# One decoder layer (Conformer mixer and gated conv-FFN): shift and scale vectors summed on VectorE, two pointwise-1 tiles per step, one LayerNorm token tile in the convolution's banks

## The chip, the cores and the metric

The kernel runs on one core of a Trainium2 chip. The metric is the device time of one execution in microseconds (us); lower is better.

## The reference, cut to what matters

One layer (DEPTH 1) of a decoder trunk, 1024 tokens by 1024 channels, everything in float32. Six vectors of 1024 values are made from `c`: shift, scale and gate for the mixer, and shift, scale and gate for the FFN.

```python
c_act = jax.nn.silu(c)
mod = c_act @ mod_w[i] + mod_b[i]                      # 1024 x 6144
sh_m, sc_m, gt_m, sh_f, sc_f, gt_f = jnp.split(mod, 6, axis=-1)
h = rmsnorm(x, norm_pre_mix[i]) * (1.0 + sc_m) + sh_m
u = h @ w1 + b1                                        # pointwise 1: 1024 -> 2048
a, gt = jnp.split(u, 2, axis=-1)
u = a * jax.nn.sigmoid(gt)                             # GLU
u = causal_dwconv(u, dw_w) + dw_b                      # depthwise, 31 taps
u = jax.nn.silu(layernorm(u, ln_g, ln_b))
y = u @ w2 + b2                                        # pointwise 2
x = x + gt_m * rmsnorm(y, norm_post_mix[i])
h = rmsnorm(x, norm_pre_ffn[i]) * (1.0 + sc_f) + sh_f
y = conv_ffn(h, ...)                                   # 1024 -> 5632, 3 taps, gate, 2816 -> 1024
x = x + gt_f * rmsnorm(y, norm_post_ffn[i])
```

## The kernel before

**Tiling.** The tokens are cut into two blocks of 512 (b = 0, 1), each of four token tiles of 128, and the channels into eight tiles of 128. A large matmul is done in three passes (`mm3`, lines 256 to 260): every operand is split into a high part and a remainder (`split`, line 241; the high part by ScalarE at L244 or VectorE at L246, the remainder by VectorE or GpSimd at L247), and high x high, high x low and low x high are added up in one PSUM bank. A matmul of 128x512 is one of the three passes.

**Memory.** PSUM has eight banks: six of the pool `bank` and two of the pool `cbank`, which the convolution accumulates in. Split weights live in four buffers `W` of 128x1024 (`pw`), so two pointwise-1 tiles' worth: each channel tile j of pointwise 1 takes two, one for the values and one for the gate. Raw weights have three buffers, `Q` tiles of 128x512 three, `Y` tiles of 128x1024 eight, `A` tiles twenty.

**The front.** `load_norm(0)` (L274) loads block 0's four token tiles, squares them on ScalarE with an accumulated sum, and scales them. Then the mixer's shift and scale come from `c` one channel tile k at a time: `channel_vectors(k)` (L137) loads two 512 KB tiles of `mod_w`; `channel_partials` (L146) multiplies them on TensorE by silu(c), eight matmuls of 128x256 in four column groups, and ScalarE copies the result; `channel_sums` (L157) adds the partitions up with two more matmuls and finishes `sh_m` and `s_m` on VectorE. `modulate_T(.., k)` (L263) transposes the normalised tokens, applies scale and shift on ScalarE, and splits the result. `pw1_step` (L296) runs the six matmuls of channel tile k for output tile j = 0. Lines 764 to 783 lay this out: all 16 tiles of `mod_w` are loaded before the weights of j = 1.

**Mixer.** Lines 801 to 823 run pointwise 1 for j = 1 to 7 of block 0 and for block 1's j = 4 to 7, 0 and 1. `glu` makes the gated result and `conv` (L335) the depthwise convolution: 7 of 31 taps go to ScalarE and GpSimd, 23 to VectorE (L355), accumulated in a `cbank`. Block 0's taps are put off in the text (`late`, L361, run at L825), while the compiler's scheduler lays the instructions of each engine in an order of its own, by readiness and then by place in the text. `ln_norm(cs0, t)` (L368) transposes one token tile of the convolution's output into two banks (L374), takes its statistics (L375) and normalises it; `ln_back` (L387) transposes back. `pointwise2` (L454) follows, with the sandwich norms in its `evacuate` (L465 to L486).

**The FFN's vectors.** `todo` (L809) holds six pieces (p, h): the mixer's gate (p = 0), the FFN's shift (p = 1) and scale (p = 2), each in two halves. `pieces()` (L787) loads four 512 KB tiles of a piece, multiplies them on TensorE (`piece_partials`, L173, matmuls at L179), and then either spreads the result over rows (`into_rows`, L224) or sums it into channel layout (`into_channels`, L186, matmuls at L190). The FFN's gate is summed on VectorE later (`row_sums`, L202 to L211).

**FFN.** `modulate_block(xs, s_f, sh_f)` (L843) needs `sh_f` and `s_f` and starts the FFN of block 0, in whose course VectorE also convolves block 1. Block 1's FFN ends with `down_strassen` (L654), whose last step accumulates each output tile into `yacc` (L664), squares it (L669), multiplies by the norm's weight (L670) and calls `finish` (L740). All DMAs go through the SP queue in order.

These lines set the order of the front:

```python
xs = load_norm(0)
ws = pw1_weights(0, DV)
chunk = [channel_vectors(k) for k in range(KD)]
...
for k in range(KD + 1):
    if k + 1 < KD:
        part.append(channel_partials(chunk[k + 1]))
    if k < KD:
        channel_sums(k, *part[k])
        hT[0][k] = modulate_T(xs, s_m, sh_m, k)
    if k > 0:
        pw1_step(bks, ws, hT[0][k - 1], k - 1)
```

## Time and profile before

| | us |
|---|---|
| median of 3 runs (lowest to highest) | 1088.54 (1087.88 to 1088.59) |
| the profiled execution | 1087.78 |
| its span, from the first to the last instruction | 1086.0 |
| TensorE busy in the span | 1059.2 (98%) |
| VectorE busy | 820.2 (76%) |
| GpSimd busy | 509.7 (47%) |
| ScalarE busy | 499.6 (46%) |

PE is TensorE's matmul stream and PEld its weight loads, DVE is VectorE, ACT ScalarE, POOL GpSimd, SP the queue that issues the DMAs. "out<-in" names tiles by the program's names. A row of grouped instructions gives its count, the busy time, the mean of one in ns, and the idle time of the engine just before them with what ended it. Matmuls overlap in the pipeline, so the time a matmul costs is the distance from its start to the next one's, not the duration in its row; the same holds on a smaller scale for the other engines. A row of the timeline gives the start, the length, the engine, the line, the operation and the count of instructions merged into it. Lines are those of the kernel before.

### The profile page before, as it was taken

The page shows a single profiled execution, that of the slowest core. Times are in us where ns is not written, and L with a number is a line of the kernel's source. Part 1 is how long each engine was busy: PE and PEld are TensorE (multiplying, and loading weights), DVE is VectorE, ACT ScalarE, POOL GpSimd, SP SyncE. Part 2 cuts the span into 40 slices and gives each one's busy share as a digit, 9 for nine tenths or more (in the row PEclk, how much of TensorE's full clock was granted, in tenths as well). Part 3 has the DMA queues.
Part 4 walks back from the last instruction along what each step waited for, and adds up shares of the span by engine and source line. Part 5 has one row for each costly group of instructions (what it writes and reads, how often), then busy time and mean ns, then how long its engine had stood idle before and what let it go on. Part 6 is the DMA issues. An engine that isn't in the chain of part 4 may idle for free.

```text
span 1086.0 us, 13033 instructions
## 1 busy us (share of the span) xinstructions
PE 1059.2 (98%) x4786; PEld 836.6 (77%) x4786; DVE 820.2 (76%) x1127; ACT 499.6 (46%) x774; POOL 509.7 (47%) x380
## 2 busy tenths in 40 slices
PE   5999999999999999999999999999999999999996
PEld 3678876778788888888887788888887888878884
DVE  3499989533899999989978673786596555965588
ACT  4495555453644544324444432455445444443443
POOL 2398876544644444444444363223257023650464
PEclk9999999999999999999999999999999999999999
DMA  9951135443422233342343253567204323033122
GB/s 377 368 195 59 59 117 194 155 135 98 155 78 97 97 97 97 93 167 90 97 166 93 92 155 97 174 213 271 91 26 155 117 97 97 20 118 116 39 77 79
DMA packets 41831, 139.00 MB, mean 128 GB/s; under 512 B 4644, under 2 KB 4644, under 8 KB 41768
## 3 DMA queue, kind: packets, MB, share of 16 engines
q1 hardware_dynamic: 41768, 138.18, 37.2%
q8 instruction: 37, 0.61, 0.2%
q14 instruction: 26, 0.21, 0.1%
HBM read 129.77 MB, written 8.39 MB: 127 GB/s over the span
## 4 chain that ended last, share of the span: by engine, by line
PE 88%; DVE 5%; DMA 3%; ACT 2%; issue 1%; POOL 1%; SPq 0%; DVEq 0%; ACTq 0%; POOLq 0%
PE bank L259 26%; PE bank L260 26%; PE bank L258 26%; PE bank L636 2%; PE bank L637 2%; PE bank L635 2%; DMA raw<-in_w 1%; PE bank L179 1%; DVE W L247 1%; DMA Af<-in_mod_ch 1%; DMA Y<-in_mod_ch 1%; DVE R L699 1%; DVE yacc L664 1%; ACT W L244 0%; DVE n L462 0%
## 5 line engine op out<-in xcount | busy, mean ns | idle before, releaser
L259 PE MATMUL bank<-A,W 128*128 128x512 f32 x960 | 379.1, 395 | 1.7 <-DVE A L247 1.7
L258 PE MATMUL bank<-A,W 128*128 128x512 f32 x960 | 378.4, 397 | 1.0 <-DVE A L246 0.7
L260 PE MATMUL bank<-A,W 128*128 128x512 f32 x960 | 378.6, 395 | 0.0
L247 POOL TENSOR_TENSOR W<-raw,W 128x1024 fp32r<-128x1024 f32 x99 | 244.4, 2470 | 271.0 <-ACT W L244 228.5
L355 DVE SCALAR_TENSOR_TENSOR cbank<-U,vecs,cbank 128x512 f32<-128x512 f32 x424 | 290.9, 749 | 9.0 <-ACT cbank L343 7.8
L258 PEld LDWEIGHTS bank<-A,W 128*128 128x128 f32 x960 | 180.1, 188 | 49.2 <-issue 1.9
L259 PEld LDWEIGHTS bank<-A,W 128*128 128x128 f32 x960 | 180.5, 188 | 45.9 <-DVE A L247 2.5
L260 PEld LDWEIGHTS bank<-A,W 128*128 128x128 f32 x960 | 180.5, 188 | 43.6 <-issue 0.8
L244 ACT ACTIVATE W<-raw 128x1024 fp32r<-128x1024 f32 x150 | 157.9, 1053 | 113.9 <-PE bank L260 71.7
L534 ACT ACTIVATE U<-bank,vecs 128x512 f32<-128x512 f32 x88 | 68.3, 778 | 193.9 <-PE bank L260 193.6
L535 DVE SCALAR_TENSOR_TENSOR U<-bank,vecs,U 128x511 f32<-128x511 f32 x88 | 65.4, 746 | 79.6 <-ACT U L534 79.4
L258 PE MATMUL bank<-W,A 128*128 128x512 f32 x304 | 121.0, 398 | 0.0
L259 PE MATMUL bank<-W,A 128*128 128x512 f32 x304 | 120.2, 395 | 0.0
L260 PE MATMUL bank<-W,A 128*128 128x512 f32 x304 | 119.0, 395 | 0.0
L540 POOL TENSOR_TENSOR U<-U,hv 128x2 f32<-128x2 f32 x44 | 12.7, 288 | 153.0 <-DVE U L535 150.0
L247 DVE TENSOR_TENSOR W<-raw,W 128x1024 fp32r<-128x1024 f32 x51 | 62.2, 1221 | 19.1 <-ACT W L244 19.1
L247 DVE TENSOR_TENSOR A<-U,A 128x512 fp32r<-128x512 f32 x73 | 69.3, 962 | 8.2 <-ACT A L244 7.7
L353 POOL TENSOR_TENSOR Q<-Q,Q 128x512 f32<-128x512 f32 x48 | 62.2, 1296 | 15.9 <-ACT Q L349 14.9
L259 PEld LDWEIGHTS bank<-W,A 128*128 128x128 f32 x304 | 57.2, 188 | 13.7 <-issue 0.5
L258 PEld LDWEIGHTS bank<-W,A 128*128 128x128 f32 x304 | 57.2, 188 | 13.7 <-issue 0.5
L260 PEld LDWEIGHTS bank<-W,A 128*128 128x128 f32 x304 | 57.2, 188 | 13.4
L536 DVE SCALAR_TENSOR_TENSOR U<-bank,vecs,U 128x510 f32<-128x510 f32 x88 | 65.3, 744 | 1.6
(154 smaller groups left out, 1188.1 us busy)
## 6 DMA issues: line engine op xcount, KB each, us to landing
raw<-in_wup SPq DMA_DIRECT2D x88, 512.0 KB, 3.2
raw<-in_w SPq DMA_DIRECT2D x40, 512.0 KB, 3.8
Y<-in_mod_hp SPq DMA_DIRECT2D x32, 512.0 KB, 5.9
raw<-in_wdn SPq DMA_DIRECT2D x22, 512.0 KB, 3.6
R<-in_wdn SPq DMA_DIRECT2D x20, 512.0 KB, 3.8
Af<-in_mod_ch SPq DMA_DIRECT2D x12, 512.0 KB, 10.2
Y<-in_x SPq DMA_DIRECT2D x8, 512.0 KB, 10.0
U<-in_x SPq DMA_DIRECT2D x16, 256.0 KB, 3.7
```

What stands on the lines that cost most here:

```text
L244: nc.scalar.activation(dst[:, 0], src, AF.Copy)
L247: split_lo[0] = lo.tensor_tensor(dst[:, 1], src, dst[:, 0].bitcast(F32), op=ALU.subtract)
L258: nc.tensor.matmul(o, l[0], r[0], start=start, stop=False)
L259: nc.tensor.matmul(o, l[0], r[1], start=False, stop=False)
L260: nc.tensor.matmul(o, l[1], r[0], start=False, stop=stop)
L353: nc.gpsimd.tensor_tensor(acp, acp, q, op=ALU.add)
L355: nc.vector.scalar_tensor_tensor(acc, ut[:, k:k + 512], tap(k), acc, op0=ALU.mult, op1=ALU.add)
L534: nc.scalar.activation(t[:, :512], bk, AF.Identity, bias=V("fb", i), scale=wk[2])
L535: nc.vector.scalar_tensor_tensor(t[:, 1:512], bk[:, 0:511], wk[1], t[:, 1:512], op0=ALU.mult, op1=ALU.add)
L536: nc.vector.scalar_tensor_tensor(t[:, 2:512], bk[:, 0:510], wk[0], t[:, 2:512], op0=ALU.mult, op1=ALU.add)
L635: nc.tensor.matmul(o, l[0], r[0], start=start, stop=False, skip_group_check=group)
L636: nc.tensor.matmul(o, l[0], r[1], start=False, stop=False, skip_group_check=group)
```

## The change

- The FFN's and the mixer's shift and scale no longer go through TensorE. `mod_w` is laid out transposed in memory, so that a tile holds 128 output channels on its partitions and all 1024 inputs along the row. silu(c) is spread over all partitions as a row (`silu_row`, or two PSUM banks in `silu_banks`), made from Sigmoid and a multiplication. A VectorE instruction multiplies a tile by that row and adds up along it (`accum_out`): two of 1024 per channel tile for the mixer (`channel_sums`), 32 of 512 for the FFN (`ffn_sums`, loaded through the three `Q` buffers, placed in the text behind `pointwise2(0, ..)`). ScalarE finishes `sh_m` and `s_m`.
- The front loads the weights of j = 0 first, those of j = 1 behind the first two channel tiles of `mod_w`, and runs pointwise 1 for j = 0 and j = 1 in the same steps (four banks). Two of the four squares of `load_norm(0)` move to VectorE, and the high part of `modulate_T` in the front to ScalarE. `load_norm(1)` moves behind the GLU of j = 1 on VectorE.
- Four of the six pieces (p = 1, 2) are gone from `todo`.
- `ln_norm` takes the convolution's two banks for token tile 2.
- At the end of block 1's FFN the last sum of a tile is written to a PSUM bank, and squared and multiplied there, rather than in `yacc`.

The diff, cut to its core (a line of "..." marks what is left out):

```diff
@@ trunk_kernel
-    nc.scalar.activation(cz[:, :, 0], V("c", 0, KD), AF.Silu)
+    sg_c = cst.tile([P, KD], F32, name="sg_c")
+    nc.scalar.activation(sg_c, V("c", 0, KD), AF.Sigmoid)
+    nc.vector.tensor_tensor(cz[:, :, 0], sg_c, V("c", 0, KD), op=ALU.mult)
...
+    def silu_row():
+        row, sg = tY(), tAf().rearrange("p a b -> p (a b)")
+        dma[0] = nc.sync.dma_start(row, rows[5:6, :].to_broadcast([P, D]))
+        def use():
+            nc.scalar.activation(sg, row, AF.Sigmoid)
+            nc.vector.tensor_tensor(row, row, sg, op=ALU.mult)
+            return row
+        return use
...
-    def channel_partials(ws):
...
-    def channel_sums(k, bk, part):
+    def channel_sums(k, ws, row):
+        d = small(2, "dot")
         for g in range(2):
-            nc.tensor.matmul(bk[:, 256 + g:257 + g], part[:, g * P:(g + 1) * P], ones[:, 0:1], start=True, stop=True)
-        nc.vector.tensor_tensor(sh_m[:, k:k + 1], bk[:, 256:257], V("mb_shm", k), op=ALU.add)
-        nc.vector.scalar_tensor_tensor(
-            s_m[:, k:k + 1], bk[:, 257:258], scb[:, 0, k:k + 1], V("pre_mix", k), op0=ALU.add, op1=ALU.mult)
+            nc.vector.scalar_tensor_tensor(
+                ws[g], ws[g], 1.0, row, op0=ALU.mult, op1=ALU.mult, accum_out=d[:, g:g + 1])
+        nc.scalar.activation(sh_m[:, k:k + 1], d[:, 0:1], AF.Identity, bias=V("mb_shm", k))
+        nc.scalar.activation(s_m[:, k:k + 1], d[:, 1:2], AF.Identity, bias=scb[:, 0, k:k + 1], scale=V("pre_mix", k))
...
+    def silu_banks():
+        cs = []
+        for h in range(2):
+            q, c = tQ(), cbank()
+            nc.sync.dma_start(q, rows[5:6, h * 512:(h + 1) * 512].to_broadcast([P, 512]))
+            nc.scalar.activation(c, q, AF.Sigmoid)
+            nc.vector.tensor_tensor(c, c, q, op=ALU.mult)
+            cs.append(c)
+        return cs
+
+    def ffn_sums(cs):
+        d = sm.tile([P, 2, 2, KD], F32, tag="dots", name=nm("dots"), bufs=1)
+        for k in range(KD):
+            for p in range(2):
+                for h in range(2):
+                    q = tQ()
+                    nc.sync.dma_start(q, mod_cf[k, p, :, h * 512:(h + 1) * 512])
+                    nc.vector.scalar_tensor_tensor(
+                        q, q, 1.0, cs[h], op0=ALU.mult, op1=ALU.mult, accum_out=d[:, p, h, k:k + 1])
+            if k % 4 == 3:
+                ks = slice(k - 3, k + 1)
+                for p, fin in ((0, fin_sh), (1, fin_s)):
+                    nc.vector.tensor_tensor(d[:, p, 0, ks], d[:, p, 0, ks], d[:, p, 1, ks], op=ALU.add)
+                    fin(d[:, p, 0, ks], ks)
...
@@ load_norm
+            if b == 0 and t % 2 == 0:
+                nc.vector.scalar_tensor_tensor(junk, xt, 1.0, xt, op0=ALU.mult, op1=ALU.mult, accum_out=ss)
+            else:
+                nc.scalar.activation(junk, xt, AF.Square, accum_out=ss)
...
@@ ln_norm
-            bk = bank()
+            bk = cbank() if t == 2 else bank()
...
@@ down_strassen
+        def close(o, t, h, z):
+            hs = slice(h * 512, (h + 1) * 512)
+            if not last:
+                return accumulate(o, t, hs, False)
+            nc.vector.tensor_tensor(z, o, yacc[t][:, hs], op=ALU.add)
+            nc.scalar.activation(yacc[t][:, hs], z, AF.Square, accum_out=ns[t][:, h:h + 1])
+            nc.vector.tensor_tensor(z, z, g_f[:, hs], op=ALU.mult)
+            zs[t, h] = z
...
@@ the order of the front
+    ws = [pw1_weights(0, DV)]
     xs = load_norm(0)
-    ws = pw1_weights(0, DV)
-    chunk = [channel_vectors(k) for k in range(KD)]
+    silu_c = silu_row()()
+    chunk = [channel_vectors(k) for k in range(2)]
+    ws.append(pw1_weights(1, DV, tY()))
+    chunk += [channel_vectors(k) for k in range(2, KD)]
...
-    bks = [bank(), bank()]
-    part = [channel_partials(chunk[0])]
+    bks = [[bank(), bank()] for _ in range(2)]
     for k in range(KD + 1):
-        if k + 1 < KD:
-            part.append(channel_partials(chunk[k + 1]))
         if k < KD:
-            channel_sums(k, *part[k])
-            hT[0][k] = modulate_T(xs, s_m, sh_m, k)
+            channel_sums(k, chunk[k], silu_c)
+            hT[0][k] = modulate_T(xs, s_m, sh_m, k, hi=nc.scalar)
         if k > 0:
-            pw1_step(bks, ws, hT[0][k - 1], k - 1)
-    glu(0, 0, bks)
-    cs0 = [conv(0, 0, POOL_TAPS)]
+            for j in range(2):
+                pw1_step(bks[j], ws[j], hT[0][k - 1], k - 1)
+    cs0 = []
+    for j in range(2):
+        glu(0, j, bks[j])
+        cs0.append(conv(0, j, POOL_TAPS))
+    with tc.issue_after(last_glu[0].ins):
+        xs = load_norm(1)
...
-    for j in range(1, KD):
+    for j in range(2, KD):
...
-            into = [(early_m, use_m), (None, into_channels(fin_sh)), (None, into_channels(fin_s))]
-            todo = [(p, h) for p in range(3) for h in range(2)]
-        if j == 1:
-            xs = load_norm(1)
+            into = [(early_m, use_m)]
+            todo = [(0, h) for h in range(2)]
...
     zs += [ln_norm(cs0, t) for t in range(2, NT)]
+    silu_c = silu_banks()
     pw1_half(1, ws, bks, 1)
...
     xs = pointwise2(0, vs, b2, g_m, x2d)
+    ffn_sums(silu_c)
     pw1(1, SHARED - 1)
     h2 = modulate_block(xs, s_f, sh_f)
```

## Rows read from the trace of the kernel before

**Rows 1.** The page, part 1: each engine's busy time, share and instruction count.

```profile
PE 1059.2 (98%) x4786; PEld 836.6 (77%) x4786; DVE 820.2 (76%) x1127; ACT 499.6 (46%) x774; POOL 509.7 (47%) x380
```

**Rows 2.** The waits on TensorE: total us, times, longest.

```profile
PE bank L267 <- DVE Y L286: 10.2, 4, 7.9
PE bank L267 <- DVE Y L486: 2.0, 1, 2.0
```

**Rows 3.** Stretches: length, each engine's busy us (x count), PE clock, DMA share, GB/s.

```profile
200.00:250.00 50.00, 49.90 (x275) 39.51 (x274) 15.15 (x39) 23.60 (x31) 20.71 (x17) 1.00 0.35 115
250.00:300.00 50.00, 47.78 (x219) 38.37 (x218) 35.54 (x53) 25.61 (x50) 25.87 (x17) 1.00 0.37 126
...
450.00:500.00 50.00, 50.00 (x216) 40.24 (x215) 45.84 (x70) 16.25 (x21) 21.66 (x9) 1.00 0.39 133
```

**Rows 4.** TensorE's timeline around one piece of the FFN's vectors.

```profile
191.10 0.95 PE L190 MATMUL bank<-ones,U 128*128 128x1 f32 x8
191.98 1.92 PE L179 MATMUL bank<-Y,cz 128*32 128x512 f32 x16
193.83 0.50 PE L258 MATMUL bank<-A,W 128*128 128x512 f32 x1
```

**Rows 5.** TensorE's groups from 0 to 67.6 us.

```profile
L258 PE MATMUL bank<-A,W 128*128 128x512 f32 x48 | 18.2, 410 | 0.7 <-DVE A L246 0.7
L267 PE MATMUL bank<-ident,Y 128*128 128x128 f32 x40 | 7.2, 310 | 10.2 <-DVE Y L286 10.2
```

**Rows 6.** ScalarE's timeline: the first modulated tile; the GLU of j = 2.

```profile
17.61 0.78 ACT L269 ACTIVATE U<-bank,sh_m,s_m 128x512 f32<-128x512 f32 x1
...
67.82 0.69 ACT L304 ACTIVATE U<-bank,vecs 128x512 f32<-128x512 f32 x1 [0.55 <-PE bank L260]
```

**Rows 7.** TensorE's timeline: the first matmuls of pointwise 1.

```profile
19.52 0.73 PE L258 MATMUL bank<-A,W 128*128 128x512 f32 x2
```

**Rows 8.** The chain that ended last: start, length (issue to landing of DMAs).

```profile
4.13 8.38 DMA Y<-in_mod_ch
...
22.77 11.67 DMA raw<-in_w
```

**Rows 9.** The page, part 5: groups of instructions over the whole span.

```profile
L247 POOL TENSOR_TENSOR W<-raw,W 128x1024 fp32r<-128x1024 f32 x99 | 244.4, 2470 | 271.0 <-ACT W L244 228.5
L355 DVE SCALAR_TENSOR_TENSOR cbank<-U,vecs,cbank 128x512 f32<-128x512 f32 x424 | 290.9, 749 | 9.0 <-ACT cbank L343 7.8
...
L244 ACT ACTIVATE W<-raw 128x1024 fp32r<-128x1024 f32 x150 | 157.9, 1053 | 113.9 <-PE bank L260 71.7
...
L247 DVE TENSOR_TENSOR W<-raw,W 128x1024 fp32r<-128x1024 f32 x51 | 62.2, 1221 | 19.1 <-ACT W L244 19.1
```

**Rows 10.** Line 210 alone: ns min/median/max of one, first and last start.

```profile
L210 DVE SCALAR_TENSOR_TENSOR U<-Y,cz,U x16: 736/751/2360, 552.7 to 586.4; 128x512 f32<-128x512 f32 x16
```

**Rows 11.** ScalarE's groups from 0 to 56.5 us: reading an accumulator.

```profile
L284 ACT ACTIVATION_READ_ACCUMULATOR Af<-Y 128x1 f32 x8 | 1.5, 187 | 0.0
```

**Rows 12.** VectorE's timeline: block 0's convolution, its first and last instructions; the second norm.

```profile
56.65 2.34 DVE L355 SCALAR_TENSOR_TENSOR cbank<-U,vecs,cbank 128x512 f32<-128x512 f32 x3 [0.98 <-ACT cbank L343]
...
200.14 0.69 DVE L357 TENSOR_TENSOR U<-cbank,Q 128x512 f32<-128x512 f32 x1
...
266.96 0.70 DVE L471 TENSOR_TENSOR bank<-bank,b 128x512 f32<-128x512 f32 x1 [8.74 <-PE bank L260]
...
288.44 1.57 DVE L486 TENSOR_SCALAR Y<-Y,n 128x1024 f32<-128x1024 f32 x1 [0.66 <-POOL n L463]
```

**Rows 13.** TensorE's timeline: the first transposes of LayerNorm.

```profile
207.82 1.97 PE L374 MATMUL bank<-ident,U 128*128 128x128 f32 x16
```

**Rows 14.** DMA issues by group: count, KB each, median us from issue to landing.

```profile
U<-in_x SPq DMA_DIRECT2D x16, 256.0 KB, 3.7
...
U<-x2d SPq DMA_DIRECT2D x16, 256.0 KB, 3.2
```

**Rows 15.** VectorE's timeline at the end: the last tiles' multiplications.

```profile
1077.56 1.51 DVE L670 TENSOR_TENSOR yacc<-yacc,g_f 128x512 f32<-128x512 f32 x1 [0.19 <-ACT bank L669]
```

More of the change, by code (lines that the diff above doesn't have):

```diff
@@ L47, in trunk_kernel @@
 @with_exitstack
-def trunk_kernel(ctx, tc, x, vec, rows, mod_ch, mod_hp, w1, w2, wup, wdn, out):
+def trunk_kernel(ctx, tc, x, vec, rows, mod_ch, mod_cf, mod_hp, w1, w2, wup, wdn, out):
     nc = tc.nc
@@ L184, in piece_partials @@
         return part
-    def into_channels(fin):
-        def use(part, h):
-            b = bank()
-            for q in range(4):
-                nc.tensor.matmul(b[:, q:q + 1], part[:, q * P:(q + 1) * P], ones[:, 0:1], start=True, stop=True)
-            fin(b[:, 0:4], slice(4 * h, 4 * h + 4))
-        return use
     def fin_sh(b, ks):
@@ L247, in split, with weights @@
         split_lo[0] = lo.tensor_tensor(dst[:, 1], src, dst[:, 0].bitcast(F32), op=ALU.subtract)
-    def weights(src, lo=nc.gpsimd):
-        raw = pr.tile([P, 1024], F32, tag="raw", name=nm("raw"))
+    def weights(src, lo=nc.gpsimd, raw=None):
+        if raw is None:
+            raw = pr.tile([P, 1024], F32, tag="raw", name=nm("raw"))
         dma[0] = nc.sync.dma_start(raw, src)
@@ L291, in trunk_kernel, with pw1_weights @@
     tail = cst.tile([P, KD, PAD], F32, name="tail")
-    def pw1_weights(j, lo=nc.gpsimd):
-        return weights(w1[j], lo), weights(w1[KD + j], lo)
+    def pw1_weights(j, lo=nc.gpsimd, raw=None):
+        return weights(w1[j], lo), weights(w1[KD + j], lo, raw)
     def pw1_step(bks, ws, h, k):
@@ L652, in down_raw, with down_strassen @@
         return raws
-    def down_strassen(ci, lo, n, ops, raws, yacc, ns=None, done=None):
+    def down_strassen(ci, lo, n, ops, raws, yacc, zs, ns=None, done=None):
         last = done is not None
@@ L726, in down_strassen, with end @@
         for t in range(2):
-            accumulate(X[t], t + 2, D2, False)
-            final(t + 2, 1, tU()[:, :512])
-        def end(banks, dt, ds, h):
+            close(X[t], t + 2, 1, cbank() if last else None)
+        def end(banks, dt, h):
             def f(t):
-                accumulate(banks[t], t + dt, ds, dt == 0)
-                final(t + dt, h, banks[t])
+                if ci == 0 and dt == 0:
+                    accumulate(banks[t], t, D2, True)
+                else:
+                    close(banks[t], t + dt, h, banks[t])
                 if last:
@@ L736, in end, with finish @@
             return f
-        sweep("A22", lambda i: raws[i][2][1, 0], Q, False, True, V, end(Q, 2, D1, 0))
-        sweep("S4", lambda i: raws[i][2][1, 1], X, False, True, V if last else G, end(X, 0, D2, 1))
-    def finish(b, yacc, ns, x2d, split_halves=True):
+        sweep("A22", lambda i: raws[i][2][1, 0], Q, False, True, V, end(Q, 2, 0))
+        sweep("S4", lambda i: raws[i][2][1, 1], X, False, True, V if last else G, end(X, 0, 1))
+    def finish(b, yacc, ns, x2d, split_halves=True, zs=None):
         def done(t):
@@ L889, in trunk_kernel @@
         ns = [small(8, "n3") for _ in range(NT)] if last else None
-        down_strassen(ci, lo, n, ops, raws, yacc, ns, finish(1, yacc, ns, x2d) if last else None)
+        zs = {}
+        down_strassen(ci, lo, n, ops, raws, yacc, zs, ns, finish(1, yacc, ns, x2d, True, zs) if last else None)
 def _layout(i):
```

46 lines of the change are left out of this document (18 added, 28 removed).

## The prediction

> **What bounds the kernel now.** I read the engines' busy time first: TensorE is busy for 98% of the span, no other engine for more than 76% [rows 1]. The waits on TensorE come next: the longest are 10.2 us for the first normalised tokens and 2.0 us for the second norm of block 0 [rows 2]. So TensorE's instruction stream sets the time, and a saving is what leaves that stream, as long as no other engine lets it run dry. The stretches show where another engine is near: VectorE has 15 of 50 us busy from 200 to 250 us and 36 from 250 to 300, but 46 from 450 to 500 [rows 3]. In that last stretch 216 matmuls take 50.00 us, so one pass of 128x512 costs 0.2315 us [rows 3]. The profiled execution took 1087.78 us, 1.78 more than its span; the median of the runs is 0.76 above it.
>
> **Pieces removed.** One piece costs TensorE 0.88 us at L190 (191.10 to 191.98) and 1.85 us at L179 (to 193.83) [rows 4]. Four pieces leave: 4 x 2.73 = 10.9 us, from a stream that has no gap there. Their four 512 KB loads each are exchanged for 32 loads of 256 KB, the same 8 MB.
>
> **The front, before.** Up to 67.6 us, just before the GLU of j = 2 [rows 6], TensorE has run 48 matmuls of each pass (the rows of the other two passes have the same count), which is j = 0, 1 and 2, and 40 transposes, 8 of them block 1's [rows 5]. Taking away j = 2 (48 x 0.2315 = 11.1 us) and 8 transposes of about 0.11 us, the work of j = 0 and 1 is done at 55.6 us.
>
> **The front, after.** Three engines feed one another; I follow channel tile k = 7.
> Transfers: the first tile of `mod_w` lands at 12.51 us, the weights sixteen transfers later at 34.44, so 512 KB take 1.37 us [rows 8]. In the new order the silu row takes that first place, and 15 tiles of `mod_w` and two of weights lie between it and the last tile: 12.51 + 18 x 1.37 = 37.2 us.
> VectorE: a dot product of 1024 is not in the trace. Its nearest row is the two-input subtraction of 128x1024, 1.22 us [rows 9]; below, I bound it by 1.13 (that row less the overlap of neighbours), above by 1.41, with an accumulator read as on ScalarE, 0.19 [rows 11]. I take 1.25. From about 15 us, when the silu row is multiplied, VectorE has 16 of these (20.0), 8 remainders of about 0.62 (5.0) and two remainders of weights (2.4): it ends at 42.4 us, the last dot product at 41.8. That is later than the transfers allow, so VectorE sets the pace.
> Then ScalarE's two small finishing steps (0.3), 1.9 us from scale-and-shift to the first matmul as at 17.61 to 19.52 [rows 6, 7], and 12 matmuls (2.8): 46.8 us. Static orders of three engines never mesh; I add 0.2 us per channel tile, 1.7 in all: 48.5.
> A new gap follows. The four weight buffers are all in use until k = 7, so j = 2's first weights are split only then: ScalarE 1.05 and GpSimd 2.47 [rows 9], against 2.1 us of remaining matmuls and 0.5 that need the high part alone. About 1.0 us.
> So 49.5 instead of 55.6: **-6.1 us**. With dot products at 1.13 and no order loss it is 45 (-10); at 1.41 and twice the order loss 54 (-2). The 128 partial and 32 summing matmuls of the front are inside this term, not beside it.
>
> **LayerNorm.** VectorE convolves block 0 from 56.65 us to 200.8 [rows 12]. The start moves to about 50.2 with the GLU, and four scalings of block 1's tokens (2.7 us) come behind it: the end moves to about 197. TensorE reaches the first transposes at 207.8 [rows 13]; less 6.1, three L179 and two L190 blocks it would be there at 194.4. So it would wait 2.7 us, unless half a pointwise-1 tile (5.6 us) that lies behind is put ahead. I take +1, bounds 0 and 3. The fourth pair of banks lets three token tiles go at once; TensorE had other work there, so I give it nothing.
>
> **The FFN's sums.** 32 instructions of 512 against a PSUM bank: 0.67 us apart like L355's (0.75 in its row) [rows 9], 21.4 us, or 27 with a read of 0.19 each [rows 11]. With three buffers the transfers set a pace too: 3.2 to 3.7 us to landing [rows 14] plus 0.75 and some 0.1 of signals, over three: 1.35 to 1.5 us each, 43 to 49 us. They can start at about 208, when LayerNorm's third tile has left the two banks, and are done by 251 to 257. They are needed when block 0's second norm is done, which ran from 266.96 to 290 [rows 12] and now ends near 273. So they fit, beside some 16 us of other VectorE work (15 in the first of the two stretches [rows 3]); what they cost is waits in VectorE's order, where an evacuation stands behind a sum whose tile has not landed, and weights standing on SP behind a load that waits for its buffer. I take +2 us, bounds 0 and 16: the upper end is VectorE's other work, not overlapped at all.
>
> **The end.** The last multiplication of `yacc` took 1.51 us [rows 15], twice the 0.75 that L355 takes for as many elements [rows 9]; in PSUM it has one SBUF input like L355, which keeps that time beside a busy GpSimd. I take -0.5, bounds -0.8 and +0.5.
>
> **Edits at nothing.** The two squares, the sigmoid of `c` and the bank of token tile 2 lie beside the transfers of the first 15 us; without that cover they would cost some 3 us. Scale and shift finished on ScalarE are in the chain above.
>
> **Sum.** -10.9 - 6.1 + 1 + 2 - 0.5 = -14.5: 1087.78 becomes 1073.3, on the median's footing 1074.
>
> **A rule that speaks against the change.** L210 is the same instruction with two SBUF inputs of float32, without the sum: its median is 0.751 us, no longer than L355's 0.749 with one input in PSUM, though its longest took 2.36 beside a busy GpSimd [rows 9, 10]. The Trainium skill, "Vector Engine (DVE) Microarchitecture Reference", section "Points that are easy to get wrong", has it that this instruction with two SBUF sources that are not bf16 runs at half throughput, as no port is left for the accumulator. By that the mixer's dot products would take twice as long, and the row without accumulation cannot exclude it.
>
> **The rivals.**
> VectorE becomes the bound between LayerNorm and the FFN. If sums come at 1.5 us each and the splits, evacuations and norms queue behind them, the last sum comes at 257, seven us behind the first evacuation of the second half (266.96 less 17), and with two waits between them the second norm ends some 9 us late, and pointwise 1 of j = 3 is all that TensorE has left. For it: [rows 12] show a chain of 23 us there already, and [rows 2] a wait at its end. Against it: [rows 3], with 49 of 100 us idle. Time: 1083.
> Dot products of 1024 at half rate: 16 x 1.2 = 19 us more on the engine that paces the front: 1093. For it nothing here but the 2.36; against it the median.
> Slower, by one mechanism: VectorE's order keeps `ffn_sums` where the text has it, behind the second norm. Then the first sum starts at about 273 and, TensorE's filler used up, it waits for 32 x 1.2 = 38 us: 1112; it decides as soon as more than 12 of the sums lie behind that norm. Against it: block 0's taps, in the text behind all of pointwise 1, start at 56.65 [rows 12], so the order follows readiness.
> The change doesn't do what it says: waits refill every slot, the conversions' gaps included: 1088.
>
> **Chances.** Forecast 0.62 (1067 to 1081); VectorE as bound 0.18; half rate 0.05; sums behind the norm 0.07; no change 0.04; better than 1067, 0.04. A difference of about 0.2% (2.2 us) is what a measurement of this kernel can tell from none. Faster: 0.62 + 0.17 + 0.04 = 0.83; within: 0.05; slower: 0.12. The range leaves out the slower cases, no change and the best: 1066 to 1086, where the first rival's upper end lies.
>
> **What would show it.** Right: j = 1's GLU near 49 us; no L190 left and 32 records of L179; TensorE with under 4 us of waits at LayerNorm and at the FFN's first transposes; the last sum before 260 us. Wrong: a dot product of 1024 over 1.5 us; a wait of TensorE over 5 us for `s_f` or for a split behind a sum; weights landing late behind a load of `Q`.

## The result: slower by 0.7%, and the profile after

The changed kernel takes **1096.45 us** (median of 4 runs, 1094.54 to 1098.5) beside 1088.21 us of the kernel before on the same chip: ratio 1.0073, 95% interval 1.0059 to 1.0087. The forecast was 1074, with a range that ended at 1086. The profiled execution took 1098.5 us, the longest of the four, so the profiles account for 10.7 us where the medians differ by 8.2.

The page, part 1, of the changed kernel [rows 1]:

```profile
PE 1044.3 (95%) x4530; PEld 832.0 (76%) x4530; DVE 865.7 (79%) x1214; ACT 502.0 (46%) x784; POOL 499.3 (46%) x378
```

TensorE is busy for 14.9 us less, as meant, yet the span is 10.7 us longer: its idle time grew by 25.6 us. Its waits from 20 to 330 us, as total, times, longest [rows 2]:

```profile
PE bank L295 <- DVE Y L317: 5.7, 1, 5.7
PE bank L286 <- ACT A L271: 5.6, 1, 5.6
PE bank L286 <- ACT Y L417: 5.1, 1, 5.1
PE bank L295 <- DVE Y L519: 4.6, 3, 2.1
PE bank L295 <- DVE Y L515: 2.4, 2, 2.2
```

In the order of time, these are the first modulated tokens (second row), block 1's first transposes (first row), the LayerNorm of block 0 (third) and the second norm of block 0 (the last two). The stretches show where TensorE thinned out, 450 to 500 us being untouched [rows 3]:

```profile
60.00:80.00 20.00, 14.04 (x66) 11.57 (x65) 19.96 (x26) 12.29 (x20) 15.64 (x14) 0.83 0.26 87
200.00:250.00 50.00, 43.69 (x210) 35.65 (x210) 29.97 (x68) 23.73 (x32) 24.57 (x21) 0.93 0.57 186
250.00:300.00 50.00, 43.16 (x184) 33.86 (x182) 40.53 (x85) 20.23 (x43) 21.53 (x15) 0.94 0.61 209
450.00:500.00 50.00, 50.00 (x216) 40.52 (x216) 46.02 (x70) 14.35 (x17) 21.64 (x9) 1.00 0.41 137
```

**A ledger.** A three-pass matmul is three matmuls of 128x512, called passes here. Every kernel runs the same 4254 passes in the same numbers per stage, so the start of the n-th one can be compared with the n-th of the kernel before. Each entry is that difference in us, from the profiled executions (+ is later). Pass 96 ends the front (j = 0 and 1), 144 stands before block 1's first transposes and 168 behind them, 696 before the last half of a pointwise-1 tile at the LayerNorm, 768 behind it, 1008 behind the second norm.

| kernel | 96 | 144 | 168 | 696 | 768 | 960 | 1008 | 4254 |
|---|---|---|---|---|---|---|---|---|
| changed | -2.6 | -1.2 | +6.6 | -1.3 | +3.9 | +3.9 | +12.6 | +12.4 |
| e1 | -3.6 | -2.2 | +1.2 | -6.7 | -0.2 | -0.3 | +7.8 | +9.4 |
| e4 | -3.7 | -2.6 | +1.6 | -5.9 | -1.4 | -1.4 | +5.8 | +6.2 |
| e2 | -4.8 | -3.4 | +3.7 | -3.9 | +8.9 | +8.9 | +10.2 | +11.1 |
| e3 | -3.5 | -2.0 | +5.7 | +5.7 | +6.8 | +6.8 | +6.8 | +6.4 |
| e12 | +0.1 | +0.1 | +0.1 | -7.7 | -2.3 | -2.3 | -2.3 | -2.0 |
| e13 | -4.1 | -2.7 | +4.9 | -3.0 | +2.0 | +2.0 | +2.0 | +1.8 |
| e14 | -4.7 | -3.7 | +0.5 | +0.5 | +1.7 | +1.7 | +1.7 | +1.5 |
| e15 | -3.9 | -2.5 | -2.3 | -2.3 | -1.2 | -1.2 | -1.2 | -1.7 |
| e18 | -4.6 | -3.1 | -3.1 | -3.2 | -3.2 | -3.2 | -2.7 | -2.5 |
| e17 | -4.9 | -3.4 | -3.2 | -3.2 | -0.5 | -0.5 | -0.1 | +0.2 |
| e19 | -4.6 | -3.1 | -3.1 | -11.0 | -4.9 | -4.9 | +3.3 | +2.6 |
| e25 | -3.9 | -2.5 | +3.2 | -4.7 | +0.5 | +0.5 | +8.5 | +9.2 |
| e23 | -4.8 | -3.3 | -3.3 | -11.1 | -3.9 | -3.7 | +1.7 | +2.8 |
| e22 | -3.1 | -1.7 | -1.7 | -9.5 | -4.0 | -4.0 | -0.2 | +0.1 |
| e24 | -5.5 | -4.0 | -3.9 | -11.5 | -5.8 | -5.8 | -2.6 | -1.9 |

Single executions scatter: the changed kernel, e2, e3, e13 and e25 have the same front and are up to 2.2 us apart at pass 96, and e16, whose front is that of the kernel before, stands at +1.8 there. So steps from one column to the next say more than a column, and the changed kernel's -2.6 is the smallest lead of its front. For the changed kernel they are: front -2.6; to pass 144 +1.4 (the split of j = 2's weights, forecast at 1.0); block 1's first transposes **+7.8**; three FFN pieces gone -7.9; LayerNorm, with the fourth piece, **+5.1**; second norm **+8.7**; the rest -0.2. The tail behind the last pass is 1.7 us shorter. Sum: +10.7. The steps say where the time was lost, not yet by what: a lead that one stage gains can come back as a wait in the next.

TensorE's timeline at two of the waits (start, length, line, and the idle time before it with what ended it):

```profile
67.41 0.55 PE L295 MATMUL bank<-ident,Y 128*128 128x128 f32 x3 [0.23 <-ACT U L337]
73.69 4.08 PE L295 MATMUL bank<-ident,Y 128*128 128x128 f32 x17 [5.73 <-DVE Y L317]
...
215.48 0.60 PE L407 MATMUL bank<-ident,U 128*128 128x128 f32 x4
221.17 0.80 PE L286 MATMUL bank<-A,W 128*128 128x512 f32 x1 [5.08 <-ACT Y L417]
221.76 0.63 PE L287 MATMUL bank<-A,W 128*128 128x512 f32 x1
222.19 0.63 PE L288 MATMUL bank<-A,W 128*128 128x512 f32 x1
```

And VectorE's, whose scaling ends the first of them; the second is ended by ScalarE (L417), behind the LayerNorm's statistics [rows 12]:

```profile
18.69 1.22 DVE L148 TENSOR_TENSOR Y<-Y,Af 128x1024 f32<-128x1024 f32 x1
...
43.26 1.23 DVE L165 SCALAR_TENSOR_TENSOR Af<-Af,Y 128x1024 f32<-128x1024 f32 x1
...
55.65 4.33 DVE L317 TENSOR_SCALAR Y<-Y,n 128x1024 f32<-128x1024 f32 x2
59.90 4.83 DVE L388 SCALAR_TENSOR_TENSOR cbank<-U,vecs,cbank 128x512 f32<-128x512 f32 x7
64.64 1.59 DVE L317 TENSOR_SCALAR Y<-Y,n 128x1024 f32<-128x1024 f32 x1
66.14 4.69 DVE L388 SCALAR_TENSOR_TENSOR cbank<-U,vecs,cbank 128x512 f32<-128x512 f32 x7
70.75 2.88 DVE L317 TENSOR_SCALAR Y<-Y,n 128x1024 f32<-128x1024 f32 x1
...
212.84 0.69 DVE L390 TENSOR_TENSOR U<-cbank,Q 128x512 f32<-128x512 f32 x1 [2.75 <-POOL Q L386]
...
276.98 0.69 DVE L221 SCALAR_TENSOR_TENSOR Q<-Q,cbank 128x512 f32<-128x512 f32 x1 [1.44 <-DMA Q<-in_mod_cf]
277.59 0.08 DVE L221 DVE_READ_ACCUMULATOR Q<-Q,cbank 128x1 f32 x1
277.59 0.69 DVE L504 TENSOR_TENSOR bank<-bank,b 128x512 f32<-128x512 f32 x1
278.93 0.69 DVE L221 SCALAR_TENSOR_TENSOR Q<-Q,cbank 128x512 f32<-128x512 f32 x1 [0.64 <-DMA Q<-in_mod_cf]
...
288.88 0.69 DVE L504 TENSOR_TENSOR bank<-bank,b 128x512 f32<-128x512 f32 x1
```

Block 1's last token tile is scaled at 70.75, among the taps. The convolution starts at 59.90 (before 56.65, forecast 50.2) and ends at 213.5 (200.8, forecast 197). The last evacuation of the second norm (L504) comes at 288.9 us; its like in the kernel before, at L471, ran at 277.5.

### The profile page after: what moved, and what is told of

It is laid out like the page before. It is cut to its first block, busy times and chain, and to the rows that moved or that the text cites. A ratio compares the mean times of both kernels' runs of the same rounds, so it can differ in the third digit from the quotient of the medians.

```text
span 1096.7 us, 12655 instructions
## 1 busy us (share of the span) xinstructions
PE 1044.3 (95%) x4530; PEld 832.0 (76%) x4530; DVE 865.7 (79%) x1214; ACT 502.0 (46%) x784; POOL 499.3 (46%) x378
## 4 chain that ended last, share of the span: by engine, by line
PE 78%; DVE 11%; DMA 3%; ACT 3%; POOL 2%; issue 2%; SPq 0%; DVEq 0%; ACTq 0%; POOLq 0%
PE bank L286 24%; PE bank L287 24%; PE bank L288 24%; DMA Q<-in_mod_cf 3%; DVE W L274 2%; ACT W L271 1%; PE bank L669 1%; PE bank L670 1%; DVE R L736 1%; PE bank L295 1%; PE bank L668 1%; DVE Y L317 1%; DVE cbank L388 1%; DVE Q L221 1%; DVE U L577 1%
## 5 line engine op out<-in xcount | busy, mean ns | idle before, releaser
L274 POOL TENSOR_TENSOR W<-raw,W 128x1024 fp32r<-128x1024 f32 x97 | 236.0, 2433 | 253.9 <-ACT W L271 211.2
L287 PEld LDWEIGHTS bank<-A,W 128*128 128x128 f32 x960 | 181.9, 190 | 44.5 <-issue 1.3
L288 PEld LDWEIGHTS bank<-A,W 128*128 128x128 f32 x960 | 181.8, 189 | 44.5 <-issue 0.8
L573 POOL TENSOR_TENSOR U<-U,hv 128x2 f32<-128x2 f32 x44 | 12.6, 287 | 152.7 <-DVE U L568 152.7
L274 DVE TENSOR_TENSOR A<-U,A 128x512 fp32r<-128x512 f32 x73 | 67.6, 939 | 9.2 <-ACT A L271 9.0
## 6 DMA issues: line engine op xcount, KB each, us to landing
Af<-in_mod_ch SPq DMA_DIRECT2D x14, 512.0 KB, 10.2
```

What stands on the lines that cost most here:

```text
L274: split_lo[0] = lo.tensor_tensor(dst[:, 1], src, dst[:, 0].bitcast(F32), op=ALU.subtract)
L287: nc.tensor.matmul(o, l[0], r[1], start=False, stop=False)
L288: nc.tensor.matmul(o, l[1], r[0], start=False, stop=stop)
L573: nc.gpsimd.tensor_tensor(t[:, 0:2], t[:, 0:2], hv[:, g, jj, :], op=ALU.add)
```

## The experiments

All ratios are to the kernel before, run on the same chip (its medians there: 1088.2 to 1090.1).

### Block 1's norm (e1, e4)

The fourth token tile waits for the buffer that the silu row holds until the last dot product, and the norms stand behind the GLU. e1 frees the buffer:

```diff
-        row, sg = tY(), tAf()...
+        row, sg = pr.tile([P, 1024], F32, tag="raw", ...), tAf()...
...
-    ws.append(pw1_weights(1, DV, tY()))
+    ws.append(pw1_weights(1, DV, tY))    # both raw weights in Y
```

> The row of silu(c) lies in a buffer of the raw weights, and step 1's two raw weights lie in the two big buffers that the row would have held and one more; so block 1's four token tiles get their buffers earlier (in the changed kernel the last waits for the row, until the last dot product at 46 us). Nothing else is altered. Theory A (the late norm of block 1 costs TensorE 7.8 us between pass 144 and pass 168, and by a late convolution the LayerNorm as well): the wait at the first transposes of block 1 (13.6 us plus 5) falls under 6, pass 168 comes 5 to 8 us earlier, and the kernel ends at 1086 to 1091. Theory B (the convolution on VectorE sets where the LayerNorm comes): pass 168 comes earlier just so, but the wait at the LayerNorm, 5.4 us now, grows by what was gained, and the end stays at 1095 to 1097.

Measured: 1096.44 us, ratio 1.0061 (1.0045 to 1.0076). Pass 168 came 5.5 us sooner and the waits there fell to 4.0, as Theory A had it; the end did not move by more than the runs scatter, as Theory B had it, though the wait at the LayerNorm itself did not grow (5.0 us). The ledger, whose end is 3.0 us sooner in the profiled execution, shows 6.5 us instead of 5.1 lost at the LayerNorm, 8.1 instead of 8.7 at the second norm, and 1.6 in the FFN, for a reason that stays open.

e4 frees the order:

```diff
-    with tc.issue_after(last_glu[0].ins):
-        xs = load_norm(1)
+    xs = load_norm(1)
```

> The loads and norms of block 1 are no longer held behind the last GLU of block 0's first two steps; the scheduler places them by itself. Theory A (order behind the GLU makes the norm late): the squares on ScalarE come before the two GLUs, the norm ends 5 us or more earlier than 73.6 us, pass 168 comes 5 to 7 us earlier, end 1087 to 1091. Theory A' (what is late is the buffer, which the row holds, not the order): the fourth token tile still lands behind the last dot product, and the end moves by under 2 us, 1094.5 to 1098. Theory B (norms ahead of the GLUs put the convolution back): convolution begins later than 59.9 us and the end is 1096 to 1101.

Measured: 1091.74 us, ratio 1.0015 (1.0006 to 1.0024), 0.7 us above Theory A's range. Two of the tiles are scaled before the GLUs, the convolution starts at 54.7 us, and TensorE's waits at block 1's transposes are, from 60 to 80 us:

```profile
PE bank L295 <- DVE U L345: 1.9, 1, 1.9
PE bank L295 <- DVE Y L317: 0.7, 1, 0.7
```

At pass 168 this is worth no more than the buffer (+1.6 beside e1's +1.2), but the taps start sooner too (54.7 us, in e1 60.6), and less is lost behind: 4.5 us at the LayerNorm and 7.2 at the second norm. At the end order counts for more than the buffer.

### LayerNorm's banks (e2)

```diff
-            bk = cbank() if t == 2 else bank()
+            bk = bank()
```

> Undoes one part: all four token tiles of the LayerNorm take the six common banks again, none the convolution's. Theory A (with two pairs of bank sources all four tiles are transposed at once, hold all banks for 7 us, and the next pointwise-1 half finds none): the wait of 5.4 us at 215.8 us shrinks to under 2, pass 720 comes 4 to 7 us earlier, end 1089 to 1092.5. Theory B (the LayerNorm is late because the convolution ends at 213.5 us instead of 200.8, and whichever bank it takes, TensorE meets it): pass 720 moves by under 2 us, since the waits move to the transposes, and the end is 1095 to 1098.

Measured: 1096.10 us, ratio 1.0058 (1.0043 to 1.0073). Theory A fell: with the common banks the wait is longer (7.0 us, for the same release of a bank by L417). What that lost, the second norm gave back (1.3 us there instead of 8.7: nine sums had begun by 230 us, one in the changed kernel). So the convolution's banks don't cause the wait; in this kernel they shorten it.

### The FFN's sums back on TensorE (e3)

```diff
...
-            into = [(early_m, use_m)]
-            todo = [(0, h) for h in range(2)]
+            into = [(early_m, use_m), (None, into_channels(fin_sh)), (None, into_channels(fin_s))]
+            todo = [(p, h) for p in range(3) for h in range(2)]
...
-    silu_c = silu_banks()
...
-    ffn_sums(silu_c)
...
```

> Undoes one part: shift and scale of the FFN are summed by TensorE again, in four pieces inside the pointwise-1 loop (10.9 us of matmuls by the profile of before), and nothing of them is left on VectorE between LayerNorm and second norm. Theory A (VectorE's 32 sums take 55 us with their waits for buffers, push back the evacuations of the second norm and cost 8.7 us there; what TensorE saved earlier was mostly lost in the LayerNorm's wait): pass 1008 no longer loses against pass 960, the wait at the LayerNorm falls by up to 5 us as TensorE comes there later, and the end is 1086 to 1092. Theory B (the wait at the second norm is inherited from the late LayerNorm and the sums are hidden): the 10.9 us come back and nothing is saved, end 1103 to 1108. In between (sums cost what the pieces cost): 1094 to 1098.

Measured: 1092.24 us, ratio 1.0023 (1.0013 to 1.0032), 0.2 us above Theory A's range. The second norm loses nothing, the LayerNorm 1.1. Putting 10.9 us of matmuls back, and taking the sums off VectorE, made the kernel 0.5% faster than the changed one.

### Pieces and sums, each left out (e12, e13)

e12 is the kernel before without the FFN's sums:

```diff
-            into = [(early_m, use_m), (None, into_channels(fin_sh)), (None, into_channels(fin_s))]
-            todo = [(p, h) for p in range(3) for h in range(2)]
+            into = [(early_m, use_m)]
+            todo = [(0, h) for h in range(2)]
+            fin_sh(V("mb_shf", 0, KD), slice(0, KD))
+            fin_s(V("mb_shf", 0, KD), slice(0, KD))
```

> The kernel before, with the four FFN pieces taken off TensorE and put nowhere: shift and scale of the FFN are their biases alone, so this leaves out these two sums. What it gains is the most that moving them could give in that kernel. Theory V (VectorE's convolution of block 0, which ends at 200.8 us in the kernel before whatever TensorE does, and the LayerNorm behind it set the time; TensorE's pieces were filler in front of them): the three pieces ahead of the LayerNorm come back as a wait there, pass 696 is 8 us earlier and pass 768 under 3 us earlier, and the end gains 2 to 5 us, 1085 to 1088 beside 1090 for the kernel before on the last chip. Theory T (TensorE's stream sets the time, as the prediction had it): 10.9 us less, 1078 to 1080.

Measured: 1087.18 us, ratio **0.9978** (0.9967 to 0.9990): 2.1 us, and 2.3 in the ledger, of the 10.9. TensorE is 7.7 us ahead at pass 696 and waits at the LayerNorm. From TensorE's timeline, VectorE's timeline and TensorE's waits:

```profile
200.37 1.69 PE L374 MATMUL bank<-ident,U 128*128 128x128 f32 x14
```

```profile
202.88 0.67 DVE L357 TENSOR_TENSOR U<-cbank,Q 128x512 f32<-128x512 f32 x1
```

```profile
PE bank L374 <- ACT Y L384: 5.2, 1, 5.2
```

The convolution ends at 203.6 us, no sooner than before (200.8), though TensorE has nothing left to do for it: it begins the LayerNorm's transposes at 200.4 us, ahead of the convolution's end and not 7 us behind it as before [rows 13]. Theory V held, in the kernel before itself and with its own banks.

e13 leaves the sums out of the changed kernel:

```diff
-    silu_c = silu_banks()
...
-    ffn_sums(silu_c)
+    fin_sh(V("mb_shf", 0, KD), slice(0, KD))
+    fin_s(V("mb_shf", 0, KD), slice(0, KD))
```

> The changed kernel without its 32 sums for the FFN and without the row of silu in the two banks; shift and scale of the FFN are their biases alone, so this leaves these two sums out. Theory A (the sums, by VectorE's order and the wait for their buffers, put the second norm back): between pass 960 and pass 1008 the 8.7 us vanish, the wait at the LayerNorm (pass 696 to 768) stays at 4 to 6, and the end is 1086 to 1090. Theory B (the second norm is late by itself, since with fewer pieces TensorE runs ahead of VectorE's chain): pass 1008 is still 4 us or more late against pass 960, end 1091 to 1096.

Measured: 1089.55 us, ratio 0.9997 (0.9986 to 1.0008). The 8.7 us at the second norm are gone to the last tenth, the 5.0 at the LayerNorm stay: Theory A.

### The parts mended together (e14, e15, e18, e17)

e14 is e3 and e4 together:

```diff
-    with tc.issue_after(last_glu[0].ins):
-        xs = load_norm(1)
+    xs = load_norm(1)
...
-    ffn_sums(silu_c)
...
```

> The changed kernel with the FFN's sums on TensorE again and block 1's loads and norms free of the last GLU. Each of the two alone took 4 to 5 us off. They sit in different stretches (60 to 80 us, and from 205 us on), so they should add up: 1087 to 1089, under the kernel before by 1 to 3 us. If the convolution on VectorE sets the LayerNorm in either, the first gain is lost there: 1090 to 1092.5.

Measured: 1088.49 us, ratio 0.9994 (0.9982 to 1.0006), in the range expected. Against the changed kernel e3 gave 0.50%, e4 0.58%, the two together 0.79%: most of it adds up.

e15 adds e1:

```diff
-        row, sg = tY(), tAf()...
+        row, sg = pr.tile([P, 1024], F32, tag="raw", ...), tAf()...
...
```

> As the run before it, and the silu row also lies in a buffer of the raw weights, so that all four token tiles of block 1 are there before the GLUs. If the buffer and the order each hold block 1's norm back: the waits at the first transposes of block 1 (3 us with the order alone, 4 us with the buffer alone) fall under 1.5 together, pass 168 comes at 74 to 76 us (76.96 in the kernel before), and the end is 1084 to 1087.5. If VectorE's convolution, begun later behind the four norms, takes it back: no better than the run before it, within 1.5 us.

Measured: **1084.65 us**, ratio 0.9960 (0.9948 to 0.9972): below both kernels. Pass 144 to 168 loses 0.1 us. Buffer and order each held the norm back, and with both mended three of the four tiles are scaled by 51.8 us, on VectorE's timeline:

```profile
51.05 0.75 DVE L325 TENSOR_SCALAR Y<-Y,n 128x1024 f32<-128x1024 f32 x1 [0.71 <-POOL n L119]
...
61.39 1.68 DVE L325 TENSOR_SCALAR Y<-Y,n 128x1024 f32<-128x1024 f32 x1
```

e18 takes the LayerNorm's part of the change out of e15:

```diff
-            bk = cbank() if t == 2 else bank()
+            bk = bank()
```

> That same fastest kernel with LayerNorm's four token tiles all in the common banks, that is without the change's part in LayerNorm. Where TensorE comes to the LayerNorm behind the convolution's end (212.6 us there, the convolution ends at 201 us), the two pairs go one after the other behind half a pointwise-1 tile each, as before, and the bank makes no difference: pass 768 within 1.5 us, ratio 0.995 to 0.997. If the convolution's banks are worth what they were in the changed kernel (5 us between pass 696 and pass 768): ratio 0.999 to 1.001.

Measured: 1083.96 us, ratio 0.9956 (0.9942 to 0.9970). From pass 696 to 768 it loses 0.0 where e15 lost 1.1: with TensorE coming behind the convolution's end, the convolution's banks are worth nothing, or a little less. In its stretches TensorE is as full as before [rows 3]:

```profile
200.00:250.00 50.00, 49.90 (x276) 39.47 (x275) 17.37 (x43) 23.68 (x34) 19.98 (x17) 1.00 0.35 111
250.00:300.00 50.00, 48.00 (x217) 39.55 (x216) 36.48 (x55) 24.15 (x46) 24.84 (x16) 0.97 0.35 121
```

e17 tries to start the dot products of e15 sooner:

```diff
-    xs = load_norm(0)
-    silu_c = silu_row()()
+    silu_c = silu_row()()
+    xs = load_norm(0)
```

> The fastest kernel so far (silu row in a raw-weight buffer, block 1's norm free of the GLU, FFN sums on TensorE; 1084.65 us beside 1089.28 of the kernel before) with the silu row loaded and made ahead of block 0's tokens. VectorE is busy without a pause from 18.4 to 44.8 us there, and its 16 dot products set the front's pace; the row's multiplication and one dot product move into its pauses before 18 us, while the tokens land 1.4 us later. Theory F (VectorE's start sets the front): the last dot product ends 0.5 to 1.5 us earlier, pass 96 comes as much earlier, ratio to the kernel before 0.9945 to 0.9958. Rival (the tokens' norms set it, 1.4 us later): pass 96 comes 0 to 1.4 us later, ratio 0.996 to 0.9975.

Measured: 1085.75 us, ratio 0.9970 (0.9959 to 0.9982), a miss. VectorE's timeline:

```profile
10.06 1.23 DVE L148 TENSOR_TENSOR raw<-raw,Af 128x1024 f32<-128x1024 f32 x1 [1.23 <-ACT Af L147]
...
17.85 1.22 DVE L165 SCALAR_TENSOR_TENSOR Y<-Y,raw 128x1024 f32<-128x1024 f32 x1
...
19.51 0.76 DVE L325 TENSOR_SCALAR Y<-Y,n 128x1024 f32<-128x1024 f32 x1 [0.43 <-POOL n L119]
```

The row is ready at 11 us, but the tokens' norms now reach to 20 us; the last dot product ends at 43.3, in e18 at 43.5. What the front gained (0.2 to 0.9 us at pass 96) was within its scatter, and 2.7 us were lost at the LayerNorm, where e15 lost 1.1, for a reason that I did not follow.

### The end alone (e16)

The kernel before with the changed `close`:

```diff
-            accumulate(Z[t], t, D1, False)
-            final(t, 0, Z[t])
+            close(Z[t], t, 0, Z[t])
...
```

> The kernel before with one part of the change alone: the last sums of block 1's FFN in PSUM. From the last large matmul to the end of the span the kernel before takes 10.5 us, the changed kernel and every one with this part 8.8 to 8.9. If this part makes that difference: 1.5 to 1.9 us less than the kernel before, ratio 0.9983 to 0.9986. If something else of the change shortens the end (the FFN's gate, the pools): within 0.5 us of the kernel before.

Measured: 1087.65 us, ratio 0.9984 (0.9975 to 0.9993), 1.7 us less. The last tiles in VectorE's timeline, here [rows 15]:

```profile
1078.64 0.70 DVE L673 TENSOR_TENSOR bank<-bank,g_f 128x512 f32<-128x512 f32 x1 [0.16 <-ACT yacc L672]
```

0.70 us instead of 1.51; and VectorE is ready for the last pair 0.1 us behind the last pass, where it was 0.6 behind.

### Order or pace of the sums (e19, e25, e23, e22, e24)

e19 is e15 with the sums on VectorE, that is the changed kernel with only block 1's norm mended:

```diff
-            todo = [(p, h) for p in range(3) for h in range(2)]
+            todo = [(0, h) for h in range(2)]
...
+    ffn_sums(silu_c)
...
```

> That same fastest kernel with the FFN's sums on VectorE as in the changed kernel; so it is the changed kernel with only block 1's norm mended in both ways. Theory V (what the removed pieces give, 7.8 us ahead of the LayerNorm, is given back there since the convolution ends no sooner, and the sums then put back the second norm by 6 to 9 us): 4 to 8 us more than the fastest, ratio 0.9995 to 1.003. Rival (the sums cost only where the LayerNorm is late already, and with block 1 in time the 10.9 us come through): 1078 to 1083 us, ratio under 0.995.

Measured: 1090.28 us, ratio 1.0013 (1.0004 to 1.0022): Theory V. TensorE is 11.0 us ahead at pass 696, keeps 4.9 behind the LayerNorm, and loses 8.2 at the second norm.

e25 moves one line of the changed kernel:

```diff
-    xs = pointwise2(0, vs, b2, g_m, x2d)
     ffn_sums(silu_c)
+    xs = pointwise2(0, vs, b2, g_m, x2d)
```

> The changed kernel with one line moved: the FFN's sums stand in the text ahead of the second pointwise layer of block 0 instead of behind it. The same 32 sums through the same three buffers, only their place in VectorE's order differs: 3 of them, not 11, stand between the evacuations of the last banks. Theory O (order: an evacuation or a step of the second norm waits behind a sum, and the sum for its load): most of the 8.7 us between pass 960 and pass 1008 goes, the end is 1088 to 1091, ratio 0.999 to 1.002. Theory L (pace of the loads: 32 at 1.7 us each end at 282 us wherever they stand, and shift and scale of the FFN wait for the last): the second norm stays 6 us or more late, ratio 1.004 to 1.008.

Measured: 1095.43 us, ratio 1.0062 (1.0049 to 1.0074), 8.0 us late at the second norm: Theory L. The sums still ended at 278.6 us.

e23 makes the same move in e19:

```diff
-    xs = pointwise2(0, vs, b2, g_m, x2d)
     ffn_sums(silu_c)
+    xs = pointwise2(0, vs, b2, g_m, x2d)
```

> The same move of the sums in the kernel with block 1's norm mended (sums on VectorE; 1090.28 us beside 1089.32, 8.2 us lost between pass 960 and pass 1008, where TensorE was 4.9 us ahead of the kernel before at pass 960). Theory O: TensorE keeps 3 to 5 us of that lead, end 1082 to 1085, ratio 0.993 to 0.9965. Theory L: ratio 0.999 to 1.002, no gain.

Measured: 1089.96 us, ratio 1.0005 (0.9994 to 1.0016): Theory L, though the second norm loses 5.4 instead of 8.2.

e22 gives the sums eleven buffers:

```diff
-                    q = tQ()
+                    q = tU()[:, :512]
                     nc.sync.dma_start(q, mod_cf[k, p, :, h * 512:(h + 1) * 512])
```

> As the run before it, and the sums' tiles go through eleven buffers (the ones the convolution's tokens leave free) instead of three. If the loads' pace counts beside the order, the sums end by 260 us instead of some 275, and the end is 1 to 3 us below the run before it; if order was all, the two agree within 1 us.

Measured: **1083.40 us**, ratio 0.9940 (0.9926 to 0.9953), 6.6 us below e23 where 1 to 3 were expected. (Its profiled execution, at 1086.2 us, was its slowest.) Line 221 by itself (ns min/median/max, first and last start), first in e23, with the time that VectorE sat idle before it:

```profile
L221 DVE SCALAR_TENSOR_TENSOR Q<-Q,cbank x32: 674/686/689, 217.7 to 269.6; 128x512 f32<-128x512 f32 x32
...
  DMA Q<-in_mod_cf: 13.5, 14
```

and in e22, where no wait stands before it:

```profile
L221 DVE SCALAR_TENSOR_TENSOR U<-U,cbank x32: 674/678/686, 228.9 to 264.4; 128x512 f32<-128x512 f32 x32
```

The same 32 instructions take 35 us instead of 52, and are over before the last four evacuations of the second norm begin at 265.5 us.

e24 puts the LayerNorm of e22 into the common banks:

```diff
-            bk = cbank() if t == 2 else bank()
+            bk = bank()
```

> As the run before it, with LayerNorm's four token tiles in the common banks. Here TensorE comes to the LayerNorm at 204 us, just when the convolution ends, as in the changed kernel, where the common banks alone cost a wait of 7.3 us for the third tile: 1 to 4 us slower than the run before it by that; within 1 us of it if the wait at the LayerNorm is the convolution's and no bank's.

Measured: 1084.39 us, ratio 0.9961 (0.9947 to 0.9974), 1.0 us above e22. From pass 696 to 768 they lose 5.5 and 5.6: here, unlike in e2, the bank makes no difference to the wait at the LayerNorm.

## Why the prediction was wrong

The forecast's terms beside the same stretches of the ledger (us; the end is the tail behind the last pass):

| term | forecast | measured |
|---|---|---|
| front, to pass 144 | -6.1 | -1.2 |
| block 1's norm | none | +7.8 |
| pieces removed | -10.9 | -7.9 and -2.6 |
| LayerNorm | +1 | +7.7 |
| FFN's sums, at the second norm | +2 | +8.7 |
| end | -0.5 | -1.7 |
| rest | none | -0.2 |
| sum | -14.5 | +10.7 |

**The premise.** It said that "TensorE's instruction stream sets the time, and a saving is what leaves that stream, as long as no other engine lets it run dry". In the kernel before VectorE is nearly as full as TensorE while it convolves block 0 (19.96 of 20 us from 60 to 80, 74.0 of 80 from 120 to 200):

```profile
60.00:80.00 20.00, 19.67 (x95) 15.48 (x94) 19.96 (x31) 18.42 (x30) 19.42 (x14) 1.00 0.61 225
120.00:200.00 80.00, 80.00 (x376) 59.21 (x375) 74.00 (x111) 42.30 (x68) 59.47 (x42) 1.00 0.44 153
```

So the sentence's own condition failed: a part of TensorE's 98% was work that fitted into the time of VectorE's convolution and norms. With nothing put in their place, four pieces of 10.9 us were worth 2.1 (e12). The pieces' own size was right: three multiplications and two of their sums, 7.3 us by the prediction's prices, gave 7.9 ahead of the LayerNorm, and the rest 2.6.

**LayerNorm, +1 with bounds 0 and 3: the step that takes the saving back.** It measured +7.7 (pass 696 to 720; what is left of the pieces then gives 2.6 back). The step compared the convolution's end with TensorE's first transposes. What TensorE needs is the release of a bank, and from the last transposes (216 us) to that (221.2) the statistics, the root and L417 take 5.1 us. And the convolution did not end at 197 but at 213.5: it started 9.7 us late, and then two scalings of block 1's tokens (4.3 us), the first statistics of the LayerNorm (1.4, and 2.4 of wait for TensorE) and a wait for GpSimd (2.8) stood among the taps. Its lateness alone is not the cause. In e1, e4, e12 and e19 it ends at 208.6, 205.4, 203.6 and 202.8 us, and a wait of 4.4 to 5.2 us is in all of them, since TensorE comes sooner too (its first transposes start 3 to 7 us ahead of the convolution's end). Wherever the pieces are on TensorE (before, e3, e14, e15, e18), it comes 3.8 to 7 us behind that end, and this wait is in none of them.

**Block 1's norm: not in the sum, +7.8.** The prediction followed `load_norm(1)` to VectorE's four scalings (2.7 us) and not to its loads, which wait for the buffer of the silu row, nor to TensorE's first transposes, which wait for the last scaling. So the moved step was followed neither to its loads nor to its last reader. e1 and e4 show the two causes, e15 both. The scalings were mis-sized too: from 55.65, 64.64 and 70.75 us on they took 4.3 (two), 1.5 and 2.8 us, 8.6 in all. GpSimd was at work beside them; that it was the reason is not tested.

**The FFN's sums, +2 with bounds 0 and 16.** +8.7, all of it the sums' (e13). The estimate of the pace, 1.35 to 1.5 us each, was a little low (54.4 us over 31 steps is 1.75), the start was further off: 227.5 us and not 208, behind the late LayerNorm. The chain of work that ended last, in the changed kernel from 225 to 305 us, by share:

```profile
by line: DMA Q<-in_mod_cf 38.5%; DVE Q L221 10.3%; DVE Y L519 6.9%; DVE Y L515 5.8%; DVE Y L506 5.6%; ACT U L427 4.6%; issue 2.9%; PE bank L295 2.8%; DVE s_f L197 2.8%; DVE bank L506 2.3%; DVE A L273 2.2%; PE bank L288 2.0%; PE bank L286 1.
```

The loads through three buffers lead it. The first rival, "VectorE becomes the bound between LayerNorm and the FFN", had the second norm "some 9 us late"; it was the right mechanism for this stage, at 0.18, though its time of 1083 lacked the other two. The rival with all the sums behind the second norm is out: the last one starts at 281.9 us, inside it.

**The front, -6.1.** That is -7.1 at pass 96 and 1.0 of gap behind it. In the profiled execution it was -2.6 at pass 96 and -1.2 at pass 144; in thirteen others with this front, or with one that differs in the row's buffer and in block 1's loads, -3.1 to -5.5 and -1.7 to -4.0. The dot products were sized right. They began late: the silu row was multiplied at 18.69 us, behind the tokens' norms, instead of about 15, and the last dot product ended at 44.5 us, forecast at 41.8. But the step that failed is that "VectorE sets the pace". TensorE's first pass starts at 25.07 us, behind the first modulated tile:

```profile
25.07 2.08 PE L286 MATMUL bank<-A,W 128*128 128x512 f32 x4 [5.55 <-ACT A L271]
```

From there it runs without a gap until both tiles are done (from 31.6 to 53.0 us it is busy for all 21.4), and it comes to the matmuls of k = 7 only at 50.2 us, when that tile had been split since 47.1. The 96 passes (22.2 us at 0.2315), seven channel tiles' transposes (some 2.5) and fourteen distances of 0.43 us at the start (some 2.8) fill the time. So the front's end was set by the first modulated tile and TensorE's own work, which the step didn't add up from there. In e17, with the row ready at 11 us and the tokens' norms later, the first pass starts at 24.2 us, in e15 at 24.8, in e18 at 24.0, so there was little to win. (The prediction's lower bound for the front, 45, is 45.9 by its own terms.)

**Half rate.** A dot product of 1024 takes 1.22 us, as the subtraction of that size does [rows 9], and 0.08 for the read of its sum. The rule of the Trainium skill ("Vector Engine (DVE) Microarchitecture Reference", "Points that are easy to get wrong") that the prediction set against the change, half throughput with two SBUF sources that are not bf16, is not borne out here for two float32 sources with a sum.

**The end, -0.5 with bounds -0.8 and +0.5.** -1.7 (e16). Beside the 0.8 us of the stretched multiplication, the waits for GpSimd's root ahead of the last step of each pair of tiles, 0.39 and 0.37 us in the kernel before, are gone; the step had not looked at them.

## What to carry to other kernels

An engine that is busy for 98% can still be filling the time of another's chain: before crediting a saving on it, take the work out in the kernel as it is and see what comes back (here 2 of 10.9 us). Follow a moved load to the buffer that it waits for and to the last of its readers. A stream of small loads through few buffers sets its consumer's pace, and with eleven buffers instead of three the same sums went from ratio 1.0005 to 0.9940, 1083.4 us, with e18 (0.9956) the fastest of these kernels.
